# Two pairs of heads taken through the RWKV-7 scan in step, with one triangular solver for both on VectorE

## The chip, the cores and the metric

The kernel runs on one core of one Trainium2 chip, on one sequence. The metric is the time of one execution on the device, in microseconds (us). Five engines work at once, each through its own queue in order: TensorE (PE, whose weight loads are listed apart as PEld), VectorE (DVE), ScalarE (ACT), GpSimd (POOL) and SyncE (SP, which here only issues DMAs).

## The reference, cut to what matters

One RWKV-7 layer and one stick-breaking attention layer, each followed by SwiGLU, over 16 learned tokens and 256 of the input (T = 272), with D = 2048, 32 RWKV heads of 64 and F = 5632, all in float32. The change lies in the RWKV layer:

```python
w = -jax.nn.softplus(-(dec_w0 + jnp.tanh(xw @ dec_w1) @ dec_w2)) - 0.5
decay = jnp.exp(-jnp.exp(w.astype(jnp.float32)))
a = jax.nn.sigmoid(a_w0 + (xa @ a_w1) @ a_w2)
g = jax.nn.sigmoid(xg @ g_w1) @ g_w2
kk = heads(k * k_k)
kk = kk * lax.rsqrt(jnp.maximum(jnp.sum(kk * kk, axis=-1, keepdims=True), 1e-24))
k = k * (1.0 + (a - 1.0) * k_a)
def step(state, inp):
    r_t, d_t, k_t, v_t, kk_t, a_t = inp
    sa = jnp.einsum('bhvk,bhk->bhv', state, -kk_t)
    state = (state * d_t[:, :, None, :]
             + sa[..., None] * (kk_t * a_t)[:, :, None, :]
             + v_t[..., None] * k_t[:, :, None, :])
    return state, jnp.einsum('bhvk,bhk->bhv', state, r_t)
_, y = lax.scan(step, s0, tuple(seq_first(t) for t in (rh, dh, kh, vh, kk, ah)))
var = jnp.mean(jnp.square(y - mean), axis=-1, keepdims=True)
y = ((y - mean) * lax.rsqrt(var + GN_EPS)).reshape(b, l, d) * gn_w + gn_b
bonus = (jnp.sum(rh * kh * r_k, axis=-1, keepdims=True) * vh).reshape(b, l, d)
out = ((y + bonus).astype(h.dtype) * g) @ w_o
```

## The kernel before, in words

**Precision.** A float32 operand is split in two parts: ACT casts it to a short form (`whi`, L217 or L170) and DVE subtracts that to get the rest (`wlo`, L218 or L171). A product of two such operands is three matmuls of 128x272 in the fast type (`mm3k`, L189 to L191). Many small products of 64x64 run in plain float32.

**Phases.** The keys of all heads and the low-rank inputs come first (up to about 163 us), among them the sum of the squares of each key over its head (`kq`, L517, one float32 product for each of 16 blocks of 128 features). Then comes the scan of 16 pairs of heads (a pair fills the 128 partitions: one head in the lower 64, one in the upper), to about 600 us, in which w_v, w_r and part of w_o are also projected. What is left of w_o (`wo_first`), the SwiGLU, the attention layer and its SwiGLU follow.

**The scan.** A sequence is 16 + 4 x 64 tokens. Within a block of 64 the recurrence is a triangular system; its inverse is built by blocks. For one pair the stages are:
- `lora` (the decay and rate of the pair: products `zw`, `za`, three ACT functions, a dozen elementwise operations that write `BK`, `ARV`, `AR0`, `B0`), `split_low` (the pair's second low-rank weights `w2h`, `w2l`), `after_v`/`after_r` (values and receptances from the stream);
- `chunk0`, `scores` (L1214: 8 products of 64x128 into two banks `ba`, `bb`, masked into `G`), `neg` (8 products into `An`), `bonus`, `tokens` (transposes into `X` and `G`), `values` (`kv`, `k0`);
- `solve` (L1259 and on: the 16x16 diagonal blocks of `G` go through DRAM to `As`, on 40 partitions; an addition and 14 pairs of dependent multiplications and additions, on POOL), `inverse` (L1275, L1278: back through DRAM into `Tt`), `left` and `right` for blocks of 16 and 32 (products `yb` L1332 and `zb` L1351, with an operation of DVE between each and the next: `Tn`, `Ys`, `Tt`), `apply` (`wa`), `trans` (`rm`, giving `Mp` and `Rh`);
- `states` (L1399, L1406: what enters the bank `cb` without a state), `step(1..4)` (L1414: the state over the blocks, with a copy of `S` by ACT between, L1416), `norm` (the variance sum `vb`, L1106, in the same `head_sums` as `bonus`; Ln and Exp on ACT, four operations on DVE, L1430 to L1436) and `gate` (`gp`).

**The order.** PE and SP run in the order in which the code is written (`manual_schedule`); the orders of ACT, DVE and POOL are set by a scheduler with costs of its own. Everything of a pair on PE is small and waits on other engines, so a generator `stream` supplies steps of the projections (one step is the three matmuls of one 128x128 block of w_v, w_r or w_o), and `fill(k)` puts k of them between the parts. The loop runs over `n`: at each turn pair A = n is in its states, M = n+1 in its inverse, B = n+2 in its scores, C = n+3 in `lora`. The PSUM banks come from three pools in turn (`rbank`), and every buffer with a name has one copy, or as many as `BUFS` says.

```python
f(6 if n == -1 else 4 if B and not A else 8 + (LEAD if n == -3 else 0))
if M:
    M.left(16)
if A:
    A.norm()
```

Of the kernel before, what the change touches and what calls it, by code (L numbers as in the profile page):

```python
# [11 lines left out]
F32 = mybir.dt.float32  # L12
# [25 lines left out]
ALIAS = {"kk": "ld"}  # L38
# [8 lines left out]
DRAIN = {13: 18 / 32, 14: 27 / 32, 15: 1.0}  # L47
# [4 lines left out]
KHEAD = 13  # L52
ASTRIDE = 2
ASTEP = 4
BUFS = {n: 2 for n in "BK AR0 G An Tt X BV0".split()}
BUFS.update(ARV=3, bv=3, pe=4)


def _consts():
# [35 lines left out]
    sel = np.zeros((128, 62))  # L95
    sel[:64, 30] = 1
    sel[64:, 31] = 1
# [21 lines left out]
NCONST = CONST_ARR.shape[1]  # L119


class Builder:
# [149 lines left out]
    def build(self):  # L272
        tc, nc = self.tc, self.nc
        with ExitStack() as ctx:
# [9 lines left out]
            for n in ("pmm", "pfr", "psc", "psd"):  # L284
                setattr(self, n, ctx.enter_context(tc.tile_pool(name=n, bufs=2, space=PSUM)))
# [76 lines left out]
    def time_mix(self):  # L362
# [15 lines left out]
        with ExitStack() as ctx:  # L378
            sp = ctx.enter_context(tc.tile_pool(name="sp", bufs=1, reuse_waits="tile"))
            self.dq = nc.sync  # L380
# [28 lines left out]
    def prologue(self, hid):  # L409
# [3 lines left out]
        with ExitStack() as ctx:  # L413
# [77 lines left out]
            kq = [self.psc.tile([32, 512], F32, name="kq", tag="sc") for _ in range(2)]  # L491
# [3 lines left out]
            def key_out(m, ps):  # L495
# [6 lines left out]
                A.activation(s2, kt, AF.Square, scale=self.vec("k_k", m))  # L502
                late.append((m, s2))
                if len(late) > 1 and m != NK // 2:
                    head_sq(*late.pop(0))
                if m == NK // 2 - 1:
                    head_sq(*late.pop(0))
                    key_norm(0, key_max(0))
# [5 lines left out]
            def head_sq(m, s2):  # L514
                o, _ = CONST["sel"]
                o += 30 - 2 * (m % 8)
                nc.tensor.matmul(kq[m // 8][:, :T], self.consts[:, o:o + 32], s2,  # L517
                                 start=m % 8 == 0, stop=m % 8 == 7)

            def key_max(i):  # L520
                t = self.rstd_p.tile([128, T], F32, name="kqs", tag="rstd")[:32]
                V.tensor_scalar(t, kq[i][:, :T], 1e-24, None, ALU.max)
# [116 lines left out]
    def scan(self, sp):  # L639
# [5 lines left out]
        self.sp = sp  # L645
        self.turn[1] = 0
        self.rot = (self.pfr, "fr"), (self.psc, "sc"), (self.psd, "sd")
# [11 lines left out]
        self.latest = self.outputs = None  # L659
        self.load_low(None, pairs[0])  # L660
        for n in range(-3, NK):
            get = lambda i: pairs.get(n + i)
            A, M, B, C = get(0), get(1), get(2), get(3)
            if n == -1:
                fill(10)
            f = fill if C else lambda k: fill(k * DRAIN[n])
            if n == NK - 1:
                self.rot = self.rot[-1:]
            if M:
                M.inverse()  # L670
            if A or C:
                self.split_low(A, C)
            if A:
# [828 lines left out]
```

## Time and profile before

| quantity | value |
|---|---|
| median of 3 runs | 2659.62 us (2659.55 to 2660.58) |
| profiled execution, its own time | 2659.44 us |
| its span in the trace | 2657.7 us (1.8 us lie around it) |
| granted PE clock, mean | 0.999 |
| PE busy | 2646.2 us, 100% |
| DVE busy | 1784.8 us, 67% |
| ACT busy | 1486.5 us, 56% |
| POOL busy | 178.7 us, 7% (all but a little in the scan) |
| in the scan, 186 to 610 us: PE, DVE, ACT, POOL busy | 418.8, 301.6, 265.5 and 176.0 of 424.0 us |
| period of a pair in the scan | 26.35 us (the `yb` of two successive pairs start at 360.20 and 386.55) |

Rows of the timeline give start and duration in us, the engine, the line, the operation with its output and inputs, the shape, and "xcount" for several in one row; in brackets, how long the engine stood idle before and what released it. The duration of a matmul is from its start to its modelled end, and successive ones overlap, so the cost of a run on PE is read from the start of one row to the start of another. Rows of the groups give the sum busy, the mean ns of one, and the idle time before.

### The profile page before, as it was taken

How to read it: one execution, taken by the hardware profiler on the slowest of the kernel's cores; microseconds unless marked ns; L12 is line 12 of the kernel's file. 1: busy time of each engine (PE TensorE's matmuls, PEld its weight loads, DVE VectorE, ACT ScalarE, POOL GpSimd, SP SyncE). 2: the span in 40 equal slices, each digit the busy share in tenths (PEclk: the TensorE clock that was granted, in tenths of full speed). 3: DMA queues.
4: the chain of work that ended last, by engine and by line, in shares of the span. 5: the costliest groups of instructions: out<-in, count | busy, mean ns of one | idle time of the engine just before them, and what ended most of it. 6: DMA issues, size and time to landing. Idle time of an engine off the chain costs nothing.

```text
span 2657.7 us, 54052 instructions
## 1 busy us (share of the span) xinstructions
PE 2646.2 (100%) x20966; PEld 2455.0 (92%) x20966; DVE 1784.8 (67%) x3603; ACT 1486.5 (56%) x3001; POOL 178.7 (7%) x493
## 2 busy tenths in 40 slices
PE   9999999999999999999999999999999999999999
PEld 8898888889999999999999999988888888888888
DVE  6677777767655555555557775788766666666665
ACT  6676666666544444444446764677555455554553
POOL 0014343440000000000000000000000000000000
PEclk9999999999999999999999999999999999999999
DMA  6444343444555555555555555434665665665655
GB/s 227 138 125 133 95 128 95 125 132 157 175 175 165 185 175 168 183 175 168 184 175 166 181 168 175 150 111 141 189 188 178 198 187 178 201 188 177 199 179 177
DMA packets 186385, 439.50 MB, mean 165 GB/s; under 512 B 58736, under 2 KB 89616, under 8 KB 186128
## 3 DMA queue, kind: packets, MB, share of 16 engines
q1 hardware_dynamic: 184784, 432.86, 52.3%
q8 instruction: 164, 2.69, 0.4%
q0 software_dynamic: 768, 2.23, 0.3%
q10 hardware_dynamic: 576, 0.96, 0.1%
q14 instruction: 93, 0.76, 0.1%
HBM read 430.24 MB, written 5.74 MB: 164 GB/s over the span
## 4 chain that ended last, share of the span: by engine, by line
PE 98%; DMA 1%; ACT 1%; POOL 0%; DVE 0%; issue 0%; SPq 0%; DVEq 0%; ACTq 0%
PE mm L194 23%; PE mm L189 17%; PE mm L191 17%; PE mm L190 17%; PE mm L193 12%; PE mm L488 1%; PE lr L575 1%; PE cb L1414 1%; PE zb L1351 1%; PE yb L1332 1%; PE wa L1362 1%; PE cb L1406 1%; PE z L1042 1%; PE lt L1055 0%; PE ba L1214 0%; PE hms L963 0%
## 5 line engine op out<-in xcount | busy, mean ns | idle before, releaser
L171 DVE TENSOR_TENSOR wlo<-raw,whi 128x512 fp32r<-128x512 f32 (+1 forms) x1432 | 968.1, 679 | 603.8 <-ACT whi L170 581.0
L170 ACT CAST whi<-raw 128x512 fp32r<-128x512 f32 (+1 forms) x1432 | 870.0, 610 | 844.4 <-PE mm L190 535.8
L189 PE MATMUL mm<-hl,whi 128*128 128x272 f32 x3328 | 968.9, 291 | 0.0
L191 PE MATMUL mm<-hl,wlo 128*128 128x272 f32 x3328 | 960.2, 289 | 0.0
L190 PE MATMUL mm<-hl,whi 128*128 128x272 f32 x3328 | 959.2, 288 | 0.0
L194 PE MATMUL mm<-hl,whi 128*128 128x512 f32 x2624 | 918.6, 394 | 0.0
L193 PE MATMUL mm<-hl,wlo 128*128 128x256 f32 x2624 | 738.0, 281 | 0.0
L189 PEld LDWEIGHTS mm<-hl,whi 128*128 128x128 f32 x3328 | 625.5, 188 | 15.0 <-issue 12.9
L190 PEld LDWEIGHTS mm<-hl,whi 128*128 128x128 f32 x3328 | 631.7, 190 | 0.6 <-issue 0.4
L191 PEld LDWEIGHTS mm<-hl,wlo 128*128 128x128 f32 x3328 | 626.0, 188 | 1.1 <-issue 0.9
L194 PEld LDWEIGHTS mm<-hl,whi 128*128 128x128 f32 x2624 | 492.4, 188 | 110.8
L193 PEld LDWEIGHTS mm<-hl,wlo 128*128 128x128 f32 x2624 | 494.1, 188 | 0.3
L218 DVE TENSOR_TENSOR wlo<-raw,whi 128x512 fp32r<-128x512 f32 (+2 forms) x156 | 108.1, 698 | 23.0 <-ACT whi L217 19.8
L217 ACT CAST whi<-raw 128x512 fp32r<-128x512 f32 (+2 forms) x156 | 93.4, 609 | 43.3 <-PE mm L190 41.5
L210 DVE TENSOR_TENSOR h<-h,mm 128x256 f32<-128x256 f32 (+1 forms) x224 | 93.9, 420 | 6.5 <-PE mm L194 6.0
L203 ACT COPY c<-mm 128x256 f32<-128x256 f32 x104 | 38.8, 373 | 75.9 <-PE mm L194 75.9
L1267 POOL TENSOR_TENSOR Tm<-Ts,As 40x14 f32<-40x14 f32 (+6 forms) x224 | 78.8, 352 | 17.5
L1269 POOL TENSOR_TENSOR Ts<-Ts,Tm 40x14 f32<-40x14 f32 (+6 forms) x224 | 76.7, 343 | 17.6
L189 PE MATMUL mm<-hi,whi 128*128 128x272 f32 x256 | 75.5, 295 | 0.0
L190 PE MATMUL mm<-lo,whi 128*128 128x272 f32 x256 | 73.7, 288 | 0.0
L191 PE MATMUL mm<-hi,wlo 128*128 128x272 f32 x256 | 73.5, 287 | 0.0
L189 PEld LDWEIGHTS mm<-hi,whi 128*128 128x128 f32 x256 | 48.1, 188 | 1.1
(292 smaller groups left out, 2345.4 us busy)
## 6 DMA issues: line engine op xcount, KB each, us to landing
raw<-w_gate SPq DMA_DIRECT2D x176, 512.0 KB
raw<-w_up SPq DMA_DIRECT2D x176, 512.0 KB
raw<-w_down SPq DMA_DIRECT2D x128, 512.0 KB
raw<-w_down SPq DMA_DIRECT2D x128, 192.0 KB
raw<-w_v SPq DMA_DIRECT2D x32, 512.0 KB
raw<-w_r SPq DMA_DIRECT2D x32, 512.0 KB
raw<-sb_w_k SPq DMA_DIRECT2D x32, 512.0 KB
raw<-sb_w_v SPq DMA_DIRECT2D x32, 512.0 KB
```

Of the source, the lines that this page charges most:

```text
L170: nc.scalar.copy(hi, part)
L171: nc.vector.tensor_tensor(lo, part, hi.bitcast(F32), ALU.subtract)
L189: mm(out, w[0], x[0], start=first, stop=False)
L190: mm(out, w[0], x[1], start=False, stop=False)
L191: return mm(out, w[1], x[0], start=False, stop=last)
L193: mm(out[:, :n], w[1], x[0], start=first, stop=False, skip_group_check=True)
L194: return mm(out, w[0], x[2], start=False, stop=last, skip_group_check=True)
L210: self.nc.vector.tensor_tensor(h, h, out[:, c:c + n], ALU.add)
L217: self.cast = nc.scalar.copy(hi, part)
L218: nc.vector.tensor_tensor(lo, part, hi.bitcast(F32), ALU.subtract)
L1267: V.tensor_tensor(t, Ts[:, 0:i, i:i + 1].to_broadcast([40, i, n]), As[:, i:i + 1, i + 1:].to_broadcast([40, i, n]), ALU.mult)
L1269: V.tensor_tensor(Ts[:, 0:i, i + 1:], Ts[:, 0:i, i + 1:], t, ALU.add)
```

## The change

**Two pairs at once.** The loop runs over `d`, and A, B, C are now lists of two pairs. A round holds `states` of both, then `step(c)` of one and of the other, with the `neg` or `chunk0` of two other pairs between; then the `scores` of both in one run of 16; one `diagonals` and one `solve` for both, on DVE and 80 partitions. `left`, `right`, `apply` and `trans` are each called for one pair and then the other, with five steps of the stream between calls. 64 steps of the stream belong to a round where 32 belonged to a pair.

**Banks.** Six PSUM banks are named by the call (`bank(name, first, second)`: the first of a round's pairs gets one, the second the other) in place of the turn over three pools.

**Engines and queues.** The solver moves from POOL to DVE, `lora`'s elementwise operations (now twelve, signs rewritten) from DVE to POOL, and `Rh` starts as a copy on POOL. The scan's DMAs through DRAM for the second pair of a round go out on POOL's queue, the first pair's on SP's; half of each pair's `s1` goes on each.

**Smaller parts.** The key sums `kq` take the split form of the squares: two 128x272 matmuls in the fast type with a cast on ACT and a subtraction on DVE, for 15 of 16 blocks. `KV0`'s product moves from `left(16)` to `left(32)`, `WV0`'s from `left(32)` to `right(32)`, and `S` follows. Some buffers share memory (`sq` with `lora`'s `ta`, `rk` with `Q`, `rs2` with `L`, `Ah` with `Tn`, `Mp` with `Ys`); `w_o`'s blocks k = 14 and 15, instead of 15 alone, are done after the scan.

```diff
-ALIAS = {"kk": "ld"}
+ALIAS = {"kk": "ld", "rs2": "L", "rk": "Q", "Ah": "Tn", "Mp": "Ys", "sq": "ta"}
-KHEAD = 13
+KHEAD = 12
+LORA = lambda nc: nc.gpsimd
...
+                if m < NK - 1:
+                    hs = pt.tile([128, 2 * T], F32R, name="hs", tag="hs", bufs=1)
+                    A.copy(hs[:, :T], s2)
+                    V.tensor_tensor(hs[:, T:], s2, hs[:, :T].bitcast(F32), ALU.subtract)
...
-                nc.tensor.matmul(kq[m // 8][:, :T], self.consts[:, o:o + 32], s2,
-                                 start=m % 8 == 0, stop=m % 8 == 7)
+                for i in range(2):
+                    nc.tensor.matmul(out, sel[:, o:o + 128], s2[:, i * T:i * T + T],
...
+        for d in range(-2, NK // 2):
+            A, B, C, N = two(d), two(d + 1), two(d + 2), two(d + 3)
...
+            for x in A:
+                x.states()
+            for c in range(1, 5):
+                for x in A:
+                    x.step(c)
+                if not B:
+                    fill(1)
+                elif c < 3:
+                    B[c - 1].neg()
+                elif c == 3:
+                    if not A:
+                        f(6)
+                    for x in B:
+                        x.chunk0()
+            for x in B:
+                x.scores()
+            if B:
+                self.diagonals(B)
+            f(6 if A else 2)
+            if B:
+                B[0].bonus()
+            for x in B:
+                x.tokens()
+            if A:
+                A[0].square()
+                A[0].variance()
+            f(2)
+            if A:
+                A[0].norm()
+            if B:
+                B[1].bonus()
+            if A:
+                A[1].square()
+            f(2)
+            if A:
+                A[1].variance()
+            f(2)
+            with tc.issue_after(self.solve(B).ins) if B else nullcontext():
+                if A:
+                    A[1].norm()
+                if C:
+                    C[0].lora(2, 3)
+                f(4)
+                if A or C:
+                    self.split_low(nth(A, 1), nth(C, 1), self.steps[-1])
+                    self.load_low(nth(B, 0), nth(N, 0))
+                f(4)
+                for x in B:
+                    x.values()
+                f(4)
+                if A:
+                    A[0].gate()
+                f(4)
+                if A:
+                    A[1].gate()
+                f(6 if A else 4)
+            if B:
+                self.inverse(B)
+            for x in B:
+                x.left(16)
+            f(5)
+            if C:
+                C[1].lora(0, 1)
+            for x in B:
+                x.right(16)
+            f(5)
...
+        self.As = self.sp.tile([80, 16, 16], F32, name="As", tag="As")
+        for i, x in enumerate(two):
+            self.dq[i].dma_start(self.As[i * 40:i * 40 + 40], x.diag(x.s1))
...
+        for i in range(1, 15):
+            n = 15 - i
+            t = Tm[:, :i * n].rearrange("p (i t) -> p i t", t=n)
+            V.tensor_tensor(t, Ts[:, 0:i, i:i + 1].to_broadcast([80, i, n]),
+                            As[:, i:i + 1, i + 1:].to_broadcast([80, i, n]), ALU.mult)
+            op = V.tensor_tensor(Ts[:, 0:i, i + 1:], Ts[:, 0:i, i + 1:], t, ALU.add)
...
+    def inverse(self, two):
+        for i, x in enumerate(two):
+            self.dq[i].dma_start(x.diag(self.s2[i]), self.Ts[i * 40:i * 40 + 40])
+        for i, x in enumerate(two):
+            x.Tt = x.big("Tt", 5, 64)
+            s2 = self.s2[i].rearrange("(a r) i t -> r i a t", r=2)
+            for r in range(2):
+                self.dq[i].dma_start(x.Tt[HS[r]], s2[r, 0:64])
```

In the changed file the same code has other lines: `mm3k` L199 to L201, splits L227 and L228, `head_sums` L1190, `parts` L1195 and L1196, `scores` L1300, `step` L1477, `square` L1488, `norm` L1498 to L1505, the solver L837 to L844.

**First place.** PE's order from the third step of the state to the scores. Here `S` is the state, `cb` the bank it enters, `ba` and `bb` the score banks of one pair. Before:

```order
L1414 MATMUL cb<-S,Mp 64x64 x2
L1414 MATMUL cb<-Rh,S 64x64 x2
L1214 MATMUL ba<-ARV,BK 128x128
L1214 MATMUL bb<-ARV,BK 128x128
L1214 MATMUL ba<-ARV,BK 128x128
L1214 MATMUL bb<-ARV,BK 128x128
L1414 MATMUL cb<-S,Mp 64x64 x2
L1414 MATMUL cb<-Rh,S 64x64 x2
```

After, from the last step of both pairs:

```order
L1477 MATMUL cb<-Rh,S 64x64 x4
L1300 MATMUL ba<-ARV,BK 128x128
L1300 MATMUL bb<-ARV,BK 128x128
L1300 MATMUL ba<-ARV,BK 128x128
L1300 MATMUL bb<-ARV,BK 128x128 x2
L1300 MATMUL ba<-ARV,BK 128x128
L1300 MATMUL bb<-ARV,BK 128x128
L1300 MATMUL ba<-ARV,BK 128x128 x2
L1300 MATMUL bb<-ARV,BK 128x128
L1300 MATMUL ba<-ARV,BK 128x128
```

The scores no longer stand in two groups of four between the steps of the state, but in one run of sixteen behind the last.

**Second place.** PE's order around the variance sum `vb`, with the buffers' numbers. Before, `vb_5917` of a pair stands behind the `yb` products of the next one (`left(16)`); ahead of these stand eight steps of the stream:

```order
L1332 MATMUL yb_5902<-Tt_5681,An_5343 64x64 x8
L1335 MATMUL yb_5902<-KV0_5558,Tt_5681 64x64 x2
L1106 MATMUL vb_5917<-hs_5860,blk_1978 128x272 x2
L189 MATMUL mm_5881<-hi_1713,whi_5882 128x272
L190 MATMUL mm_5881<-lo_1714,whi_5882 128x272
L191 MATMUL mm_5881<-hi_1713,wlo_5883 128x272
```

After, `vb_4386` is the second pair's sum of a round; the first pair's, `vb_4345`, stands two steps of the stream ahead of this piece:

```order
L1190 MATMUL bonus_4363<-hs_4096,blk_2033 128x272 x2
L199 MATMUL mm_4269<-hl_787,whi_4288 128x272
L200 MATMUL mm_4269<-hl_787,whi_4288 128x272
L201 MATMUL mm_4269<-hl_787,wlo_4289 128x272
L199 MATMUL mm_4269<-hl_794,whi_4288 128x272
L200 MATMUL mm_4269<-hl_794,whi_4288 128x272
L201 MATMUL mm_4269<-hl_794,wlo_4289 128x272
L1190 MATMUL vb_4386<-hs_4371,blk_2034 128x272 x2
```

Between the two sums stand two steps, a `bonus` sum and two more steps. ACT's order at the same place, before:

```order
L1111 CAST hs_5860<-sq_5785 128x272
L1177 COPY V0_1_1971<-mm_5598 128x16
L1178 COPY ARV_5826<-mm_5598 128x4x64
L217 CAST whi_6053<-raw_5603 128x512
L217 CAST whi_6084<-raw_5666 128x512
L1430 ACT_TABLE_LOAD
L1430 ACTIVATE rs2_5920<-vb_5917,dv_66 128x272
L217 CAST whi_6116<-raw_5666 128x512
L1431 ACT_TABLE_LOAD
L1431 ACTIVATE rs2_5920<-rs2_5920 128x272
```

and after:

```order
L1361 COPY X_4338<-tv_4327 128x4x128
L1498 ACT_TABLE_LOAD
L1498 ACTIVATE rs2_4354<-vb_4345,dv_66 128x272
L227 CAST whi_4576<-raw_4032 128x512
L1499 ACT_TABLE_LOAD
L1499 ACTIVATE rs2_4354<-rs2_4354 128x272
L1488 ACTIVATE sq_4369<-y_4224 128x272
L1195 CAST hs_4371<-sq_4369 128x272
```

The operand of the second sum, `hs_4371`, is now made on ACT behind the whole norm of the first pair; before, a pair's `hs` stood ahead of its own norm, with nothing of another norm in front.

**Third place.** DVE's order. Before, while POOL solves, DVE's row around the norm is mixed with the splits `wlo` of the stream:

```order
L218 TENSOR_TENSOR wlo_4692<-raw_4241,whi_4691 128x512
L1337 TENSOR_TENSOR Ys_4551<-yb_4540,consts_64 128x256
L1341 TENSOR_TENSOR WV0_4553<-yb_4540,BV0_3902 128x64
L218 TENSOR_TENSOR wlo_4723<-raw_4304,whi_4722 128x512
L1352 TENSOR_TENSOR Tt_4319<-Tt_4319,zb_4582 128x256
L218 TENSOR_TENSOR wlo_4755<-raw_4304,whi_4754 128x512
L1432 TENSOR_TENSOR sq_4423<-rs2_4558 128x272
```

After, contiguous rows of DVE from the end of the first pair's norm into the solver:

```order
L1503 SCALAR_TENSOR_TENSOR rs2_4354<-sq_4357,rs2_4354 128x272
L1504 TENSOR_TENSOR y_4220<-y_4220,rs2_4354 128x272
L1505 SCALAR_TENSOR_TENSOR y_4220<-y_4220,dv_66,bv_3417 128x272
L1196 TENSOR_TENSOR hs_4371<-sq_4369,hs_4371 128x272
L1337 TENSOR_TENSOR bv_4366<-V0_1_2027,bonus_4363 128x16
L1339 TENSOR_TENSOR bv_4366<-ARV_3835,bonus_4363 128x256
L837 TENSOR_TENSOR Ts_4395<-As_4266,consts_64 80x256
L842 TENSOR_TENSOR Tm_4396<-Ts_4395,As_4266 80x14
L844 TENSOR_TENSOR Ts_4395<-Ts_4395,Tm_4396 80x14
```

and, after 24 more rows of L842 and L844, from the end of the solver on:

```order
L842 TENSOR_TENSOR Tm_4396<-Ts_4395,As_4266 80x14
L844 TENSOR_TENSOR Ts_4395<-Ts_4395,Tm_4396 80x14
L1501 TENSOR_TENSOR sq_4429<-rs2_4426 128x272
L1213 TENSOR_SCALAR ld_4444<-ld_4444 128x272
L1502 SCALAR_TENSOR_TENSOR sq_4429<-vb_4386,sq_4429 128x272
L228 TENSOR_TENSOR wlo_4474<-raw_3944,whi_4473 128x512
```

No split of the stream stands among the 29 operations of the solver. `wlo_4474` is read first by the third matmul of the stream's 17th step of the round; between `vb_4386` and that step stand 18 matmuls of the stream and the six of `zw` and `za`.

More of the change, by code (lines that the diff above doesn't have):

```diff
@@ L46 @@
 LEAD = 4
-DRAIN = {13: 18 / 32, 14: 27 / 32, 15: 1.0}
 PSTEP = 8
@@ L744, in scan @@
+            f(5)
+            for x in B:
+                x.trans()
+            f(5)
         fill(100)
```

372 lines of the change are left out of this document (166 added, 206 removed).

## The prediction

> **What bounds the kernel now.** I read the page's engine shares and its chain first, then the chain of waits through one pair of the scan, and then the timelines of PE, ACT and DVE there.
>
> ```profile
> PE 2646.2 (100%) x20966; PEld 2455.0 (92%) x20966; DVE 1784.8 (67%) x3603; ACT 1486.5 (56%) x3001; POOL 178.7 (7%) x493
> PE 98%; DMA 1%; ACT 1%; POOL 0%; DVE 0%; issue 0%; SPq 0%; DVEq 0%; ACTq 0%
> 186.00:610.00 424.00, 418.80 (x5653) 374.98 (x5651) 301.58 (x768) 265.51 (x629) 175.95 (x477) 1.00 0.43 119
> 360.20 0.61 PE yb L1332 x16
> 386.55 0.61 PE yb L1332 x16
> ```
>
> PE is the bound everywhere, in the scan too (third line: PE busy 418.80 of 424.00 us, then PEld, DVE, ACT, POOL). A pair takes 386.55 − 360.20 = 26.35 us, and its PE hardly waits. So the change can win only by PE doing the same work in less time, and it loses whatever it makes PE wait. No engine's total forbids the change; what counts is the order in which a round's dependent work comes due.
>
> **Gain 1: fewer runs of small products.** What a run costs beyond its products is seen where one stands inside the stream:
>
> ```profile
> 362.59 0.29 PE L191 MATMUL mm<-hi,wlo 128*128 128x272 f32 x1
> 362.81 0.68 PE L1351 MATMUL zb<-Ys,Tn 64*64 64x64 f32 x16
> 363.65 0.29 PE L190 MATMUL gp<-hg0l,w2h 128*128 128x272 f32 x1
> 376.34 0.29 PE L1406 MATMUL cb<-G,X 128*64 128x64 f32 x4
> 376.46 0.29 PE L1406 MATMUL cb<-X,G 128*64 128x64 f32 x4
> ```
>
> From L191 to L190 there are 1.06 us by starts, in which two stream matmuls (this L191 and an L189 between) take 2 x 0.125. (Their durations of 0.29 overlap; 2646.2 us over 20966 products in the page's first line is 0.126 a product, and a step of the stream has three.) The run costs 0.81. Its 16 entries by the spacing within a run (four in 376.46 − 376.34 = 0.12, so 0.029 each) are 0.47; 0.34 is left for there and back, 0.17 a switch. In the order of before I count 22 switches a pair (six runs alone in the stream with two each, ten among states, steps, scores, `neg` and `tokens`, as the first place of the order shows), 44 for two; after it 25 for two. 19 x 0.17 = 3.2 us a round, 8 rounds: **−26 us** (ends −30 and −20, for a switch of 0.20 or 0.13).
>
> Two small things cancel: before, `kv` runs inside `yb` and now stands alone; and the state's copy, for which PE waited, is now covered by the other pair's products.
>
> ```profile
> 365.87 0.62 PE L1332 MATMUL yb<-Tt,An 64*64 64x64 f32 x14
> 366.89 0.40 PE L189 MATMUL mm<-hi,whi 128*128 128x272 f32 x1
> 377.63 0.32 ACT S L1416
> ```
>
> `yb` with `kv` is 40 entries in 1.02 us, against 0.14 + 40 x 0.029 = 1.31 for two runs: 0.29 lost a pair. Of the 0.32 of the copy (377.63), for which the products of the next step wait, about 0.25 is now filled by the other pair's products. I put the two together at zero; with either alone the term moves by 0.3 x 16 = 5 us.
>
> **Gain 2: the key sums.** Before, one plain float32 product; after, two fast matmuls of 0.125.
>
> ```profile
> 53.22 0.28 PE L191 MATMUL mm<-hl,wlo 128*128 128x272 f32 x1
> 53.43 0.65 PE L517 MATMUL kq<-xi,consts 128*32 128x272 f32 x2
> 54.24 0.29 PE L190 MATMUL mm<-hl,whi 128*128 128x272 f32 x1
> 40.00:163.00 123.00, 123.00 (x798) 106.92 (x798) 82.19 (x175) 89.18 (x208) 1.20 (x9) 1.00 0.41 128
> ```
>
> 54.24 − 53.22 less two stream spacings is 0.77; 0.77 − 0.25 = 0.52, 15 times: **−8 us** (−6 if a block is caught by its cast). The added cast and subtraction (about 0.43 each, rows below) lie beside PE: DVE has 41 and ACT 34 us to spare in those 123. If that cover went, each block would cost up to 0.9.
>
> **Loss 1: the second variance sum.** In the new order 16 matmuls stand from the first sum `vb` to the second, 2.0 us of PE. The second needs `hs` of its pair, which ACT and DVE now make behind the first pair's norm (and `sq` has one buffer, which that norm still reads). The prices are those of the same operations before:
>
> ```profile
> 360.75 1.28 ACT L1430 ACT_TABLE_LOAD   x1
> 362.04 0.49 ACT L1430 ACTIVATE rs<-vb,dv 128x272 f32<-128x272 f32 x1
> 362.79 0.62 ACT L217 CAST whi<-raw 128x512 fp32r<-128x512 f32 x1 [0.26 <-PE mm L190]
> 363.43 1.28 ACT L1431 ACT_TABLE_LOAD   x1
> 364.72 0.43 ACT L1431 ACTIVATE rs<-rs 128x272 f32<-128x272 f32 x1
> 365.19 0.48 DVE L1432 TENSOR_TENSOR sq<-rs 128x272 f32<-128x272 f32 x1 [0.62 <-ACT rs L1431]
> 365.95 0.40 DVE L1433 SCALAR_TENSOR_TENSOR sq<-vb,sq 128x272 f32<-128x272 f32 x1
> 366.38 0.45 DVE L1434 SCALAR_TENSOR_TENSOR rs<-sq,rs 128x272 f32<-128x272 f32 x1
> L1422 ACT ACTIVATE sq<-y 128x272 f32<-128x272 f32 x16 | 6.9, 431 | 0.4
> L1111 ACT CAST hs<-rs 128x272 fp32r<-128x272 f32 x16 | 6.7, 420 | 12.8 <-DVE rs L1186 12.8
> L1112 DVE TENSOR_TENSOR hs<-sq,hs 128x272 fp32r<-128x272 f32 x16 | 7.0, 436 | 0.1
> ```
>
> A copy of `X` ahead (about 0.5, an estimate by the 0.42 to 0.49 rows), then 1.28 + 0.49 + 0.62 + 1.28 + 0.43 = 4.1 on ACT, 0.48 + 0.40 + 0.45 with gaps 1.4 on DVE until `sq` is free, 0.43 + 0.42 on ACT, 0.44 on DVE: 7.3 to 7.4 us. PE waits 7.4 − 2.0 = 5.4 a round: **+43 us** (3.9 if copy and cast of the stream are already done: +31; 5.7 if another split stands between: +46). Behind the waiting `vb` in PE's queue stands everything: the stream too, whose splits are ready.
>
> **Loss 2: the solver in front of the splits.** DVE's 29 operations of the solver depend on one another. They have no row on DVE with 80 partitions; the nearest in size are two small operations, and POOL's own bound it from above:
>
> ```profile
> L1341 DVE TENSOR_TENSOR WV<-yb,BV 128x64 f32<-128x64 f32 x16 | 3.4, 215 | 0.0
> L1170 DVE TENSOR_TENSOR B<-kk,Q 128x16 f32<-128x16 f32 x14 | 2.4, 168 | 0.0
> L218 DVE TENSOR_TENSOR wlo<-raw,whi 128x512 fp32r<-128x512 f32 x133 | 94.8, 717 | 20.4 <-ACT whi L217 17.4 <-PE mm L190 1.9
> L1267 POOL TENSOR_TENSOR Tm<-Ts,As 40x14 f32<-40x14 f32 (+6 forms) x224 | 78.8, 352 | 17.5
> ```
>
> The 14 to 56 elements lie between the two rows: 0.19, and 0.03 to the next dependent one (366.38 − 366.35 above), say 0.225 for 28 of them, 0.44 for the first: 6.75 us. From `hs` of the second pair to the split that PE needs next: `bv` 0.4, solver 6.75, about 1.15 for two operations of the norm (0.48, 0.40 above) and one of `lora`, `wlo` 0.7: 9.0. PE has 28 matmuls from that sum to the first use of `wlo`, 3.5 us. It waits 5.4, in each of 8 solves (the first, without states, waits for its `As` much alike): **+43 us**. Ends: half the shorter row an operation (0.084) gives a solver of 2.8 and a wait of 1.5, +12; POOL's 0.35 gives 10 and 8.6, +68. I take the DVE rows, being the same engine and size. That the two waits add is no double count: the second starts from the end of the first.
>
> **Loss 3: behind the solver.** DVE then has norm, splits and `G` in a heap, while POOL runs twelve operations of `lora`, and the second pair's `Tt` reads stand on POOL's queue behind these.
>
> ```profile
> 361.30 0.73 POOL L1262 TENSOR_TENSOR Ts<-As,consts 40x256 f32<-40x256 f32 x1 [13.41 <-DMA As<-s]
> 361.45 1.13 DVE L218 TENSOR_TENSOR wlo<-raw,whi 128x512 fp32r<-128x512 f32 x1
> 362.11 0.54 POOL L1267 TENSOR_TENSOR Tm<-Ts,As 40x14 f32<-40x14 f32 x1
> 362.73 0.21 POOL L1269 TENSOR_TENSOR Ts<-Ts,Tm 40x14 f32<-40x14 f32 x1
> ```
>
> Side by side the two slow each other: `wlo` 1.13 against 0.72, POOL's 40x14 0.54 beside it and 0.21 after. Twelve of POOL at about 0.73 are some 9 us. What of this PE sees, the gate's weights or the second `Tt` late, I take as 2.5 us in 7 rounds: **+17** (0 and 5 us: 0 and +35).
>
> The Trainium skill ("SBUF — State Buffer", section "SBUF: two separate sides") speaks against this move: it says that a DVE operation with two inputs in SBUF and a GpSimd operation that reads SBUF hold a port pair as an exclusive lock, and that the other one blocks for the whole instruction. By it all of `lora` on POOL would be serial with DVE's splits, which is a rival below, at 2787; the 1.13 and 0.54 agree with it in kind, and no row shows POOL with 128x272.
>
> **Loss 4: the clock after a gap.** In the trace a wait for `Tt` of 2.55 us near the end is followed by:
>
> ```profile
> 589.39 2.55 DMA Tt<-s
> 592.00:594.00 2.00, 2.00 (x26) 1.84 (x27) 2.00 (x7) 0.56 (x2) 0.00 (x0) 0.92 0.95 297
> 594.00:596.00 2.00, 2.00 (x14) 1.75 (x15) 0.92 (x3) 1.99 (x3) 0.00 (x0) 0.50 1.07 391
> 596.00:598.00 2.00, 2.00 (x24) 1.88 (x22) 1.93 (x6) 0.21 (x1) 0.00 (x0) 0.73 0.71 269
> ```
>
> The granted clock 0.92, 0.50, 0.73 costs 2 x (0.08 + 0.50 + 0.27) = 1.7 us. Once a round: **+14** (0 if no gap brings it, 27 if both gaps of a round do). I take once, since the second gap comes some 4 us behind the first, within the same slow stretch. The Trainium skill ("TensorE: Matmul & The Clock Gate", section "What's actually happening") gives an idle window of about 3.4 us before half clock; here it came after 2.55, so the measurement decides. By the page's window both waits of 5.4 would count, +27, and the sum would be 2755.
>
> Sum: −26 − 8 + 43 + 43 + 17 + 14 = **+83**, on 2659.4 of the profiled execution (0.2 under the median, so no correction): **2742 us**. All good ends: −30 − 8 + 31 + 12 = +5, 2665; all bad: −20 − 6 + 46 + 68 + 35 + 27 = +150, 2810. `wo_first`'s second late block, the aliases and named banks I price at nothing: the stream has the same matmuls, and the waits above are longer than any for a bank.
>
> **Rivals.**
> - *The dependent work keeps up* (faster). The two losses need chains of 7.4 + 9.0 = 16.4 us against 5.5 of PE. The gains are 34/8 = 4.25 a round, so it turns at a chain of 9.75. That wants table loads that are done ahead of `vb` (2.6 off) and solver operations at about 0.08 (4 off). For it: PE's matmuls start at half their durations, so DVE's might. Against: 366.38 follows 365.95, on which it depends, by the full 0.43. Time: 2659.4 − 26 − 8 = 2626.
> - *Only the first wait*: the solver on DVE ends in about 3 us, so that its wait falls to under 2 (the +12 end) and the heap behind it with it: 2742 − 31 − 14 = 2697. For it: half the shorter row; against: the 0.43 from 365.95 to 366.38.
> - *POOL and DVE block each other* (slower still): twelve operations of 0.73 are 8.8 us that DVE's splits wait in full instead of 2.5, (8.8 − 2.5) x 7 = +44, and with a cold clock after both gaps +13: 2786 to 2800. It decides if `wlo` beside `lora` takes well over the 1.13 above. This is the rule of the Trainium skill's page "SBUF — State Buffer" (same section); the one pair of rows that shows it has DVE slowed by half, not stopped.
> - *The switches don't get cheaper* (0.17 is waiting, not mode): 2768, inside the range.
> - *No change*: waits of 4.25 a round by chance.
>
> **How the numbers follow.** Both waits, 2700 to 2775: 0.58. The port case, above: 0.14. One wait only: 0.10. Faster: 0.15. Within 0.2% (5.3 us, about what a measurement can tell here): 0.03. Slower: 0.58 + 0.14 + 0.10 = 0.82. The range of 2668 to 2810 leaves out the faster case and the no-change case, 0.18, and a little above.
>
> **What would show it.** Right: PE idle of 4 to 6 us before the second `vb` of a round, released by DVE's `hs`; another of about 5 before an `mm` L201, released by `wlo` L228, while DVE runs 29 operations L837 to L844 in 6 to 7 us; granted clock at half behind them; 8 rounds, each near 2 x 26.35 − 4 + 14 = 62 to 63 us; `kq` at 0.25. Wrong: rounds near 49 us with PE busy through, DVE's solver in 3 us, or ACT making the second `hs` ahead of the table loads; or waits elsewhere, as for the second pair's `Tt`.

## The result and the profile after: slower, past the end of the range

The changed kernel takes 2843.23 us (median of 4 runs, 2841.32 to 2846.33) against 2659.59 us: a ratio of 1.0691 (95% interval 1.0678 to 1.0704), 184 us more. Forecast were 2742 us and a range to 2810. The direction held, the size did not. The profiled execution has a span of 2841.7 us. The first line of its page and its chain:

```profile
PE 2671.2 (94%) x20966; PEld 2494.3 (88%) x20966; DVE 1802.2 (63%) x3689; ACT 1491.4 (52%) x3016; POOL 211.7 (7%) x301
PE 87%; DMA 4%; DVE 3%; POOL 2%; ACT 2%; issue 1%; SPq 1%; DVEq 0%; POOLq 0%; ACTq 0%
```

PE is busy in 94% where it was in 100%, and the chain now goes through DMAs, DVE, POOL, ACT and SP's queue. What PE waited for between 160 and 800 us (engine, line, what it waited for: us in total, times, longest):

```profile
PE yb L1394 <- DMA Tt<-s: 84.2, 16, 13.5
PE vb L1190 <- DVE bv L1339: 43.9, 7, 8.8
PE mm L201 <- DVE wlo L228: 21.3, 8, 7.0
PE vb L1190 <- ACT hs L1195: 4.7, 1, 4.7
```

Two of the waits are those of the prediction (the second `vb`, and the split `wlo`). The largest, for `Tt`, stood there only as a small part of another term. The scan's windows, of the kernel before and then of the changed one (window, its length and PE busy; the clock is the third number from the end):

```profile
160.00:780.00 620.00, 614.80 (x7261) 568.52 (x7260) 430.69 (x1018) 377.91 (x846) 177.30 (x480) 1.00 0.47 136
```

```profile
160.00:780.00 620.00, 461.00 (x5787) 428.12 (x5788) 328.80 (x875) 273.94 (x650) 210.05 (x288) 0.85 0.31 87
```

PE's idle time there rose from 5.2 to 159.0 us, and the mean clock fell to 0.85. By windows of 1 us from 0 to 840 us, PE's idle time is 166.9 against 7.5, and its busy time times (1 − clock) sums to 53.9 against 1.7. That is 159.4 + 52.2 = 211.6 us of loss, where the spans differ by 184.0. So by this account the same work at full clock takes some 27.6 us less than before: the gains are there, and the losses are more than seven times as large.

**One round, followed back from the `yb` that waits.** These are pieces of the chain of waits in the changed kernel:

```profile
418.40 0.59 ACT X L1361
425.92 0.33 DVE bv L1339
426.25 0.34 DVE Ts L837
433.97 0.60 DVE wlo L228
435.56 4.81 POOL k L1227
443.15 0.77 POOL kk L1232
444.23 0.27 SPq L798
446.48 9.87 DMA s<-Ts
457.06 2.51 DMA Tt<-s
459.61 1.97 PE yb L1394 x30
```

The solver ends at 433.1, 6.8 us after 426.25. Yet SP issues the write of its result (`s<-Ts`) only at 446.48, because in SP's written order the load of the next pair's `rn` (L798) stands ahead. Its buffer comes free only when POOL has done `kk` (L1232), the fifth of `lora`'s operations there, and POOL's first one alone (`k`, L1227) took 4.81 us. Three loads of weights of 512 KB and two smaller ones then also go out ahead of the write, which lands 9.87 us after its issue. Before, the same two DMAs went out 2.0 us apart with no weights between:

```profile
373.90 0.31 SPq L1275 DMA_DIRECT2D s<-Ts  x1
375.94 1.28 SPq L1278 DMA_DIRECT2D Tt<-s  x2
```

**The clock.** Windows of the changed kernel in that round: behind the waits at `vb` (426 to 434), at `wlo` (436) and for `Tt` (462).

```profile
426.00:428.00 2.00, 1.60 (x7) 1.63 (x8) 1.76 (x9) 1.42 (x3) 0.00 (x0) 0.50 0.02 4
428.00:430.00 2.00, 2.00 (x11) 2.00 (x11) 1.72 (x9) 1.99 (x4) 0.00 (x0) 0.50 0.00 0
430.00:432.00 2.00, 2.00 (x14) 2.00 (x13) 1.71 (x9) 0.42 (x2) 0.00 (x0) 0.72 0.00 0
432.00:434.00 2.00, 0.27 (x3) 0.06 (x1) 1.84 (x9) 0.90 (x3) 0.38 (x1) 1.00 0.00 0
436.00:438.00 2.00, 2.00 (x26) 1.75 (x27) 2.00 (x4) 0.93 (x3) 2.00 (x1) 0.51 0.00 0
462.00:464.00 2.00, 2.00 (x11) 2.00 (x11) 0.30 (x2) 0.62 (x1) 0.00 (x0) 0.50 0.19 78
```

The clock is at half in three stretches of this round, one behind each wait, and stays there until some 3 to 6 us after PE resumes. Between 160 and 800 us there are 23 such stretches. Each of PE's gaps of 2.1 us or more there has one behind it, except one of 2.81 us at `wlo`, which ends at 278.64.

**The gains.** In the changed kernel two `zb` of two pairs stand in one run, and `kq` in pairs of fast products:

```profile
394.14 0.28 PE L201 MATMUL mm<-hi,wlo 128*128 128x272 f32 x1
395.66 0.39 PE L199 MATMUL mm<-hi,whi 128*128 128x272 f32 x1
54.95 0.29 PE L201 MATMUL mm<-hl,wlo 128*128 128x272 f32 x1
55.24 0.39 PE L539 MATMUL kq<-hs,selr 128*128 128x272 f32 x1
55.47 0.28 PE L199 MATMUL mm<-hl,whi 128*128 128x272 f32 x1
```

40 entries of `zb` take 395.66 − 394.14 − 0.13 = 1.39, where two runs of 16 alone took 1.62 and eight more entries 0.23 by the spacing: 0.46 less for the two pairs, near the 0.34 of the two switches saved. The first `kq` of this block costs 0.52 − 0.13 = 0.39, not 0.13.

### The profile page after: what moved, and what is told of

Read it like the earlier page. It is cut to its first block, busy times and chain, and to the rows that moved or that the text cites. A ratio compares the mean times of both kernels' runs of the same rounds, so it can differ in the third digit from the quotient of the medians.

```text
span 2841.7 us, 54127 instructions
## 1 busy us (share of the span) xinstructions
PE 2671.2 (94%) x20966; PEld 2494.3 (88%) x20966; DVE 1802.2 (63%) x3689; ACT 1491.4 (52%) x3016; POOL 211.7 (7%) x301
## 4 chain that ended last, share of the span: by engine, by line
PE 87%; DMA 4%; DVE 3%; POOL 2%; ACT 2%; issue 1%; SPq 1%; DVEq 0%; POOLq 0%; ACTq 0%
PE mm L204 21%; PE mm L199 15%; PE mm L201 15%; PE mm L200 15%; PE mm L203 11%; DMA s<-Ts 2%; PE lr L598 1%; PE mm L499 1%; POOL k L1227 1%; DVE Tm L842 1%; DVE Ts L844 1%; PE yb L1394 1%; DMA Tt<-s 1%; PE zb L1410 1%; PE wa L1427 1%
## 5 line engine op out<-in xcount | busy, mean ns | idle before, releaser
L181 DVE TENSOR_TENSOR wlo<-raw,whi 128x512 fp32r<-128x512 f32 (+1 forms) x1432 | 968.2, 679 | 593.2 <-ACT whi L180 575.0
L180 ACT CAST whi<-raw 128x512 fp32r<-128x512 f32 (+1 forms) x1432 | 870.0, 610 | 839.6 <-PE mm L200 528.0
L199 PE MATMUL mm<-hl,whi 128*128 128x272 f32 x3328 | 975.7, 293 | 0.2 <-ACT whi L227 0.2
L201 PE MATMUL mm<-hl,wlo 128*128 128x272 f32 x3328 | 970.6, 292 | 0.2 <-DVE wlo L228 0.2
L200 PEld LDWEIGHTS mm<-hl,whi 128*128 128x128 f32 x3328 | 642.5, 193 | 5.5 <-DVE hl L271 5.4
L199 PEld LDWEIGHTS mm<-hl,whi 128*128 128x128 f32 x3328 | 637.2, 191 | 5.1 <-issue 0.5
L201 PEld LDWEIGHTS mm<-hl,wlo 128*128 128x128 f32 x3328 | 636.8, 191 | 0.7 <-DVE wlo L228 0.4
L204 PEld LDWEIGHTS mm<-hl,whi 128*128 128x128 f32 x2624 | 492.4, 188 | 111.9
L227 ACT CAST whi<-raw 128x512 fp32r<-128x512 f32 (+1 forms) x154 | 92.5, 612 | 186.1 <-PE mm L200 119.1
L228 DVE TENSOR_TENSOR wlo<-raw,whi 128x512 fp32r<-128x512 f32 (+1 forms) x154 | 113.3, 754 | 110.6 <-ACT whi L227 107.3
L1394 PE MATMUL yb<-Tt,An 64*64 64x64 f32 x512 | 28.7, 260 | 84.4 <-DMA Tt<-s 84.2
L1394 PEld LDWEIGHTS yb<-Tt,An 64*64 64x64 f32 x512 | 24.3, 169 | 88.8 <-issue 79.3
L201 PE MATMUL mm<-hi,wlo 128*128 128x272 f32 x256 | 77.2, 302 | 21.1 <-DVE wlo L228 21.1
L199 PE MATMUL mm<-hi,whi 128*128 128x272 f32 x256 | 78.8, 308 | 0.0
L201 PEld LDWEIGHTS mm<-hi,wlo 128*128 128x128 f32 x256 | 50.6, 198 | 22.6 <-DVE wlo L228 22.6
```

The source lines that it names most:

```text
L180: nc.scalar.copy(hi, part)
L181: nc.vector.tensor_tensor(lo, part, hi.bitcast(F32), ALU.subtract)
L199: mm(out, w[0], x[0], start=first, stop=False)
L200: mm(out, w[0], x[1], start=False, stop=False)
L201: return mm(out, w[1], x[0], start=False, stop=last)
L204: return mm(out, w[0], x[2], start=False, stop=last, skip_group_check=True)
```

## The experiments

All are edits of the changed kernel, unless another is named. The theory after the result was: PE stands because of orders in queues, above all SP's, and each stand brings half clock. The rivals were that the solver itself ends too late, that the waits add up singly, and that POOL's part is not in the way.

**load_late: `load_low` behind the write of the solver's result.**

```diff
                     self.split_low(nth(A, 1), nth(C, 1), self.steps[-1])
-                    self.load_low(nth(B, 0), nth(N, 0))
...
             if B:
                 self.inverse(B)
+            if A or C:
+                self.load_low(nth(B, 0), nth(N, 0))
```

> load_low, whose DMA of rn waits until lora on POOL has read the old rn, is written behind inverse, so that SP issues the solver's result (s<-Ts) without that wait; three loads of weights still stand ahead of it. In the changed kernel SP issued rn at 443.95 us of one round, s<-Ts at 446.5, it landed 9.9 us later, and PE waited some 10.5 us for Tt. Theory Q (SP's queue order holds the result back): s<-Ts is issued between 435 and 441 there, still lands late behind weights, the wait for Tt falls from 84 to 30-55 us, time 2795-2820. Rival P (the second pair's Tt, behind lora on POOL's queue, sets the time as well, ready at about 454.5 there): no more than 5 us a round are won, 2805-2843. Rival S (the solver's late end alone): no change, 2835-2850.

Measured: 2816.25 us, ratio 1.0593 (1.0575 to 1.0611), 27 us less than the changed kernel. PE's wait in all, SP's queue in one round, and there the second pair's read of `Tt` (from POOL's queue) and PE's wait for it:

```profile
PE yb L1395 <- DMA Tt<-s: 50.3, 26, 5.9
425.19 0.36 SPq L851 DMA_DIRECT2D s<-Ts  x1
430.53 1.27 SPq L856 DMA_DIRECT2D Tt<-s  x2
433.95 8.17 DMA Tt<-s
440.00 0.44 PE L1395 MATMUL yb<-Tt,An 64*64 64x64 f32 x2 [5.67 <-DMA Tt<-s]
```

As theory Q had it: without the wait for `rn` the wait for `Tt` falls from 84 to 50 us, and the write still lands 5.3 us after its issue, behind weights. But the time lies in rival P's range too, and P's part is there: some 33 of the 50 us stand ahead of the second pair's `yb`. That pair's read is issued on POOL behind the twelve operations of `lora` (433.25) and lands 8.17 us later. So two queues held `Tt`, SP's the longer, and POOL's next behind it.

**inv_early: the solver's DMAs directly behind the solver.**

```diff
-            with tc.issue_after(self.solve(B).ins) if B else nullcontext():
+            solved = self.solve(B) if B else None
+            if B:
+                self.inverse(B)
+            with tc.issue_after(solved.ins) if B else nullcontext():
...
-            if B:
-                self.inverse(B)
             for x in B:
                 x.left(16)
```

> The solver's DMAs (write, and read of Tt) of both pairs are written directly behind the solver, ahead of the stream's loads, of load_low, and on POOL ahead of most of lora. Theory Q: the result leaves at about 433.6 us of the round looked at in place of 446.5, lands in 2-3 us, Tt is there at about 440 before PE's need at 449; the wait for Tt goes from 84 to under 10 us, and part of the slow clock behind it: 2735-2765. Rival (weights are now late instead, since SP stands for the solver before it loads): half of that comes back as a wait for wlo or whi, 2790-2820. Rival S: no change, 2835-2850.

Measured: 2786.5 us, 1.0477 (1.0462 to 1.0493), 57 us less. Its waits and SP's rows:

```profile
PE zb L1411 <- DVE Ys L1400: 26.4, 5, 5.5
PE yb L1395 <- DMA Tt<-s: 4.1, 1, 4.1
414.08 0.30 SPq L851 DMA_DIRECT2D s<-Ts  x1
416.10 1.27 SPq L856 DMA_DIRECT2D Tt<-s  x2
425.64 0.53 SPq L799 DMA_DIRECT2D rn<-rkd  x1
```

The edit moves the DMAs of both queues, SP's and POOL's. The write now lands in 2.0 us and the wait for `Tt` is gone (4.1). A third of it came back as the rival had it: `rn` (425.64) still waits for `lora` on POOL, the next weights go out behind it, their split comes late on DVE, and `Ys` stands behind that split. The time fell between the two expectations.

**both: the two together.**

> inv_early and load_late together: the solver's DMAs directly behind the solver, and load_low, whose rn waits for lora, behind the stream's loads. inv_early alone left a new wait of 26 us (zb for Ys, which stood on DVE behind a split whose weights SP could issue only after rn). Theory Q: that wait goes, none comes for it, 2735-2765. Rival (SP's stand at the read of Tt delays the weights all the same): 2775-2790.

Measured: 2752.23 us, 1.0351 (1.0335 to 1.0366), 91 us less than the changed kernel, within theory Q. What is left:

```profile
PE vb L1192 <- DVE bv L1341: 43.7, 7, 8.6
PE mm L201 <- DVE wlo L228: 21.8, 8, 7.0
PE yb L1396 <- DMA Tt<-s: 4.6, 1, 4.6
```

`zb` no longer waits. So half of the change's loss was the place of a few DMAs in the queues of SP and POOL. By windows of 1 us the idle time is 90.3 and the clock's loss 37.9.

**squares: the second pair's square ahead of the first pair's norm.**

```diff
             if A:
                 A[0].square()
+                A[1].square()
                 A[0].variance()
...
-            if A:
-                A[1].square()
             f(2)
             if A:
                 A[1].variance()
```

> The second pair's square and its hs are made ahead of the first pair's norm, so that the second variance sum does not wait. The prediction's sum took the two waits (vb, then the split behind the solver) as independent terms that add. Theory A (they add): the 49 us of vb go and nothing comes, 2785-2800. Theory C (one chain: norm of the first pair, bv, solver, split; PE only meets it at another place): the wait at vb falls from 49 to under 5, the wait for wlo rises from 21 to 55-70, the time moves by less than 15: 2828-2845.

Measured: 2837.54 us, 1.067 (1.0654 to 1.0685). Neither theory was tested, since the wait did not go:

```profile
PE vb L1189 <- DVE bv L1338: 44.4, 7, 8.3
```

`hs` now stands ahead of the norm on ACT and DVE, and `vb` still waits as long, for `bv`. The second pair's `vb` is in bank 5, and so is the `bonus` sum of another pair just before, which DVE's `bv` must read first. `bv` stands behind the first norm in DVE's order. In the changed kernel both came late; this is DVE's row of `hs` in the round above:

```profile
425.40 0.44 DVE L1196 TENSOR_TENSOR hs<-sq,hs 128x272 fp32r<-128x272 f32 x1
```

It ends at 425.84, `bv` at 426.25. So by these times `hs` held `vb` for all but the last 0.4 us, and with `hs` early `bv` alone holds it nearly as long.

**vbsq: the same, and the second pair's `vb` in bank 1 for pairs 0 to 11.**

```diff
-        out = self.bank(name, 4, 5)[:, :T]
+        out = self.bank(name, 4, second)[:, :T]
...
-        self.vb = self.head_sums("vb", self.b.blk[1], self.squares)
+        self.vb = self.head_sums("vb", self.b.blk[1], self.squares, 1 if self.p < 12 else 5)
```

> squares moved ahead of the norm as before, and the second pair's vb in bank 1 (for the pairs 0 to 11) in place of bank 5, where the bonus sum of another pair waits to be read by DVE's bv, which stands behind the first norm. In squares alone the wait at vb stayed at 44 us, so the bank, not hs, would hold it. Theory B (bank): the wait at vb falls to 8-15 us (two rounds keep bank 5). Of the time: theory C (one chain, solver and splits stand where they stood) the wait for wlo rises by as much and the time is 2825-2843; theory A (waits add) 2795-2812.

Measured: 2829.24 us, 1.0643 (1.0626 to 1.0661).

```profile
PE mm L201 <- DVE wlo L228: 63.1, 8, 10.1
PE vb L1189 <- DVE bv L1338: 8.3, 1, 8.3
```

Theory B and theory C held: with `hs` early the named bank was what held `vb`, and taking it away too moved the wait to `wlo`, which rose from 21 to 63 us. The two are one chain, which PE meets in two places. Of the 48.6 us at `vb`, 39 went, and 42 came at `wlo`. The 14 us won against the changed kernel came elsewhere: 9 at `Tt`, and 11 from less half clock (42.7 by the windows of 1 us).

**lora_dve: `lora` back on DVE** (`LORA = lambda nc: nc.vector`).

> lora's elementwise operations go back to DVE. In the changed kernel POOL's first one of a round took 4.8 us in five rounds (0.6 to 1.0 in others), ending when DVE's run of operations ended. Theory L (the port: POOL's operation stands while DVE has operations back to back, and SP's rn behind it): rn is free 4-6 us sooner in a round, the wait for Tt falls by 25-40 us, part of it given back by splits that stand behind 12 operations of 0.2-0.5 us on DVE: 2800-2835. Rival D (DVE is the bound of that stretch, POOL's 4.8 us is not in the way): the splits' wait grows by 4-5 us a round, 2850-2890.

Measured: 2813.5 us, 1.0577 (1.0561 to 1.0592), 30 us less.

```profile
PE yb L1394 <- DMA Tt<-s: 45.9, 14, 6.6
```

Theory L: `rn` comes free sooner, and the wait for `Tt` falls by 38 us; the 12 operations on DVE cost `wlo` only 2 us more (23.5), and `yb` now also waits 7.7 us for DVE's `Tt`.

**first_dve: only the first operation of `lora` of a round's first pair on DVE.**

```diff
-        E.tensor_scalar(k2, ta, self.vec("k_a"), self.vec("oka"), ALU.mult, ALU.add)
+        (E if self.e else V).tensor_scalar(k2, ta, self.vec("k_a"), self.vec("oka"), ALU.mult, ALU.add)
```

> The changed kernel with lora's first operation (k2 = ta times vector plus vector) of a round's first pair on DVE, the other eleven on POOL. In the changed kernel this operation took 4.8 us on POOL in six rounds, and ended 0.45 us after DVE's run of back-to-back operations ended. Theory L (port: whichever operation of POOL comes into DVE's run stands until the run ends): the next operation of POOL (a product of k2, or ta, or kk) takes 3-5 us in its place and ends 0.2-0.8 us after DVE's run. Rival (it is that operation's own cost, or POOL's start after a DMA): no operation of POOL there over 1.8 us, rn is free some 4 us sooner.

There is one run of it, of which only the trace is used. POOL's row and DVE's row in one round (span 2835.6 us):

```profile
434.69 4.58 POOL L1228 TENSOR_TENSOR k<-k,kt 128x272 f32<-128x272 f32 x1 [1.79 <-DVE k L1227]
435.57 3.07 DVE L228 TENSOR_TENSOR wlo<-raw,whi 128x512 fp32r<-128x512 f32 x5
```

Now the next operation of POOL takes 4.58 us, in five rounds alike, and ends at 439.27, 0.63 us after DVE's run of splits (to 438.64). The wait for `Tt` stays at 80.2 us. It is not the operation, but where it falls: POOL stands while DVE has operations back to back. The Trainium skill ("SBUF — State Buffer", section "SBUF: two separate sides") calls it an exclusive lock of the port pair that the two share, held for a whole instruction. The trace agrees in kind (4.58 us for one operation) and adds that a run of DVE's, with no gap, kept POOL out from one instruction to the next, here through seven or eight of them.

**engines_back: the solver on POOL, `lora` on DVE, the splits free of the solver** (`issue_after` taken out).

> The solver on POOL (80 partitions, once for two pairs) and lora's elementwise operations on DVE, the stream's splits not held behind the solver; DMAs and order of PE and SP as in the changed kernel. The solver should take 10-11 us on POOL against 6.8 on DVE. Theory (the DVE solver in front of the splits costs the wlo wait): wlo falls from 21-23 to under 5 us, Tt comes 2-4 us later a round than with lora alone on DVE: 2790-2825. Rival (POOL stands for DVE's runs of operations, port): the solver takes over 14 us on POOL and the wait for Tt grows by more than 30 us: over 2840.

Measured: 2789.11 us, 1.0489 (1.0474 to 1.0505), 54 us less, just under what was expected.

```profile
PE yb L1396 <- DMA Tt<-s: 50.1, 13, 10.0
PE mm L201 <- DVE wlo L228: 1.0, 2, 0.8
```

The wait for `wlo` is gone (1.0). Three things changed at once; with `lora` alone on DVE (`lora_dve`) it stayed at 23.5, so it was the solver on DVE with the order that holds the splits behind it. Which of these two would do alone is not shown. On POOL the solver took 12.7 us (403.0 to 415.7 in one round) against 6.8.

**busy: 90 products that keep PE from standing ahead of `left(16)`.**

```diff
+            if A and C:
+                B[0].busy(90)
             for x in B:
                 x.left(16)
...
+    def busy(self, n):
+        spare = self.b.bank(0, "spare")
+        for i in range(n):
+            self.PE.matmul(spare[:, :T], self.b.blk[1], self.b.hg[0][0], start=True, stop=True)
```

> The changed kernel with 90 matmuls of 128x272, whose result nobody reads, ahead of left(16) in six rounds, where PE otherwise stands 13.1 us for Tt; 90 x 0.125 = 11.3 us, so they end before Tt comes. Theory K (the granted clock falls to half because PE stands, and comes back some 5 us after it resumes): the clock stays 1.00 through left(16), 2.5-3 us a round are won, 2822-2832 us. Rival (the half clock has another cause, or the added products delay yb): 2840-2860.

Measured: 2837.85 us, 1.0668 (1.0653 to 1.0683), 5 us less. PE's timeline, and windows:

```profile
443.47 11.44 PE L1198 MATMUL spare<-hg0h,blk 128*128 128x272 f32 x90
457.14 0.47 PE L1401 MATMUL yb<-Tt,An 64*64 64x64 f32 x2 [2.23 <-DMA Tt<-s]
```

```profile
446.00:454.00 8.00, 8.00 (x67) 8.00 (x66) 2.88 (x7) 1.56 (x3) 0.66 (x1) 1.00 0.70 230
462.00:464.00 2.00, 2.00 (x12) 2.00 (x11) 0.69 (x1) 0.55 (x1) 0.00 (x0) 0.57 0.02 6
```

Neither expectation held for the time: the added products only fill what PE stood before, and the clock's loss, by the windows of 1 us, fell from 53.9 to 48.2. While PE runs, the clock stays at 1.00 (446 to 454). In four of the six rounds PE then stands 1.8 us for `Tt` or not at all, and no half clock follows there, as theory K had it: it is PE's standing that brings it. In the other two, the 2.1 and 2.2 us that were left brought it all the same, in this round until about 463, as long after PE resumed as behind 13.1 us. What was won there was partly lost at other places, as behind `wlo`, where some stretches are longer than in the changed kernel; why stays open.

**before_kq: the kernel before, with the key sums alone in the split form.**

> The kernel before with the key sums alone changed to the split form (two 128x272 matmuls in the fast type for 15 of 16 blocks). The prediction's term: 0.52 us less for each of 15, -8 us, 2650-2654. Rival (the cast and the subtraction catch PE, or the switch stays): within 2 us of before, 2657-2662.

Measured: 2654.9 us, ratio 0.9985 (0.9976 to 0.9994): 4.0 us less, by the interval 1.6 to 6.4. Half of the 8, as the rows of `kq` above say: 0.77 − 0.39 − 0.13 = 0.25 a block, 15 blocks, 3.8. Not all blocks are alike: in four of them both products fall among those of the low-rank inputs and last 0.49 each. Why the first of the two costs more is not known.

**best1 and best3: attempts at the change without its waits.** best1 has `both`, `vbsq` and `engines_back`, the solver's DMAs of both pairs on POOL's queue, and 12 steps of the stream moved ahead of `left(16)`. best3 also has `values` ahead of `lora`, the second `k0` in bank 4 and the solver's scratch in another buffer.

> Engines back, squares and bank as in vbsq, the solver's DMAs of both pairs on POOL's queue directly behind the solver, load_low behind, and 12 steps of the stream moved from between left, right, apply and trans to ahead of left(16). Theory W (the change's loss is waits and their clock, and the cheaper switches are real): waits under 15 us in all, 2625-2660. Rival R (scores, DRAM, solver, DRAM, Tt is a chain of some 27 us that a round's 22 us between scores and left can't hide): waits of 4-8 us a round with half clock behind, 2680-2740.

> best1 with its two new waits taken away: values (kv, k0) written ahead of lora, the second k0 in bank 4, and the solver's scratch in another buffer than KV0's. In best1 PE stood 27 us for k0 (its bank held za, which ACT read late) and 27 us for gp (w2h, behind a copy of KV0 whose buffer the solver held). Theory W: those 54 us and a part of the 38 us of slow clock go: 2670-2695. Rival (other waits take their place, as in squares): 2720-2765.

Measured: best1 2759.96 us, 1.0381 (1.0365 to 1.0396); best3 2770.36 us, 1.0415 (1.0401 to 1.043). The first two rows are PE's waits in best1, the last is best3's:

```profile
PE k L1377 <- ACT ta L1218: 27.4, 6, 4.6
PE gp L199 <- ACT w2h L808: 26.5, 7, 4.9
PE yb L1396 <- DMA Tt<-s: 48.5, 23, 8.4
```

Neither time lies in a range that was given; the rivals were nearer, by 20 and 5 us. In best1 the old waits fell (`Tt` to 11.7, `wlo` to 1.1) and two new ones came, from a named bank and a shared buffer. In best3 these fell (`k0` to 14), and `Tt` (48.5) and `wlo` (20.9) came back. Rival R reads this as a chain from the scores to `Tt` that a round's order does not hide, and that shows at whichever instruction of PE comes first; no run tests that by itself. No version here beats the kernel before; `both` with 2752 is the nearest.

## Why the prediction was wrong, point by point

- **The sum.** 184 us against 83. Of the 101 that were missing, the wait for `Tt` is 67 and the clock 38; the gains fell short by 6, and losses 1 and 2 came out 16 smaller.
- **Gains.** The switches: forecast −26; the traces leave 27.6 for both gains, and `before_kq` gives 4.0 of it to the key sums, so about −24, near the forecast; no run changes the switches alone. The key sums: −8 forecast, −4 measured; the step that failed took both fast products at the stream's 0.125, while the first costs 0.39.
- **Loss 1, the second `vb`.** +43 forecast, 48.6 measured (43.9 + 4.7). The chain that was added up is there: from the copy of `X` (418.40) to the end of `hs` (425.84) it took 7.4 us, against 7.3 to 7.4. What the sum left out is a second hold of nearly the same length, bank 5 through `bv`, also behind that norm. "Named banks I price at nothing" cost only the last 0.4 us of a round here, but it meant that mending `hs` alone leaves the wait (`squares`). That the two waits add held: they are one chain, as the sum had it, and `vbsq` only moved the wait (69.9 us for both in the changed kernel, 72.4 in `vbsq`).
- **Loss 2, the solver ahead of the splits.** +43 forecast, 21.3 measured: 7.0 in the first round, 2.1 to 2.8 in six others. The chain held here too, 8.7 us from the end of `hs` to that of `wlo` (434.57) against 9.0, with the solver at 6.8 against 6.75; `lora_dve` and `engines_back` together put the wait on the solver and the order behind it. Less was left at `wlo` because `vb` had already waited for `bv`, just ahead of the solver (0.5), and PE did the products up to the split at half clock, which took some 2.4 us of the same time (the windows from 426 to 432).
- **Loss 3, behind the solver.** This is the step that failed most: 2.5 us in 7 rounds, +17, at most +35; measured 84.2 for `Tt`. I looked at POOL's queue for the second pair and not at SP's for the first. There the write of the result stands behind `rn`, which waits for `lora`, and behind three loads of weights. I had read in the trace of before that write and read are 2.0 us apart, and did not ask what the new order puts between. POOL's queue was priced too low as well: with SP's wait for `rn` gone it still cost some 33 us (`load_late`). `inv_early` and `both`, which move the DMAs of both queues, took that loss away.
- **The rival of the ports** named the mechanism that lengthens it (4.8 us for one operation), but as a delay of DVE's splits. It was POOL that stood, and SP behind POOL.
- **Loss 4, the clock.** 1.7 us a gap was near (1.6 to 3.4), but I counted one gap a round, +14; there were 23 in all, 52.2 us. I took the second gap as within the first one's slow stretch, but the clock was back at 1.00 between them (432 to 434). I also read the 2.55 us of the transfer as PE's wait; PE itself stood 1.81 us there (589.53 to 591.34). The page's window of 3.4 us in the Trainium skill ("TensorE: Matmul & The Clock Gate", section "What's actually happening") does not fit either: gaps of 2.2 us (`busy`) brought half clock. With it as a rule I would have counted two gaps.
- **The direction** was right, and the condition put for the faster case, a chain of under 9.75 us a round, was far from met: 16.2 us from 418.40 to 434.57 in the round shown, where the sum had 16.4.

## What to carry to other kernels

When a step moves, write down for each DMA it issues what stands ahead of it in that queue, and what each of those waits for; here one load that waited for a buffer held a result that had been ready for 13 us. Waits that lie on one chain don't go singly: moving one shows the next, so price the chain from its start to PE's last possible use, and look for a second hold at the same place. And count the gaps of PE, not only their sum, since nearly every gap over 2 us brought its own stretch at half clock here.

## What the runs showed of the hardware that was not expected

- POOL can stand through a run of DVE's operations: 4.58 to 4.81 us for operations of 128x272 that mostly take 0.6 to 1.0, ending 0.45 to 0.63 us after DVE's run.
- A write of 40 KB in one queue landed 2.0 us after its issue with no weights ahead, 5.3 to 6.0 behind three loads of 512 KB that had gone out over some 4 us (`load_late`, `lora_dve`), and 9.4 to 10.2 where these and two smaller ones had gone out within 2.5 us (five rounds of the changed kernel).
- The granted clock fell to half behind gaps of PE of 1.81 us (the kernel before), 2.1 to 2.5 and 13 us (the changed kernel), and came back 3 to 7 us after PE resumed; such a stretch cost 1.6 to 3.4 us. No length divides them: behind 2.81 us in the changed kernel and 1.76 and 1.78 us in `busy` the clock stayed at 1.00.
